# RWKV element work in pairs of 512 columns, token shift partly on ScalarE, attention banks emptied by ScalarE

## The chip, the cores and the metric

One core of a Trainium2 chip (trn2) runs the whole kernel in one launch. The metric is device time in microseconds (us): 1360.03 us, the median of 3 runs (1355.95 to 1360.05). Engine names are those of the profile: PE is TensorE, DVE is VectorE, ACT is ScalarE, POOL is GpSimd, SP is SyncE, which issues most of the transfers.

## The reference, cut to what matters

One decoder layer for 256 positions and width 2048, all in float32:

```
p = rms_norm(h, norm_mix) @ w_in                       # 16 RWKV heads x 64, and attention
p = p + (shift(p) - p) * mu                            # token shift, RWKV columns only
r, k, v, xw, xa, xg = split(p)
decay = exp(-exp(-softplus(-(w0 + tanh(xw) @ w_decay_up)) - 0.5))
a = sigmoid(a0 + xa @ a_up);  g = sigmoid(xg) @ g_up
kk = k * k_k / max(|k * k_k|, 1e-12);  k = k * (1 + (a - 1) * k_a)
state = state * decay + (state @ -kk) (kk * a)^T + v k^T ;  y = state @ r      # 256 steps
yn = layer_norm(y) ;  bonus = sum(r * k * r_k) * v
y_rwkv = (yn + bonus) * g
y_att = sparse attention (indexer, top 64 of 256 keys)
h = h + [y_rwkv, y_att] @ w_mix_out ; h = h + cross attention ; h = h + relu(..)^2 MLP
```

## The kernel before, in words

All projections go through `gemm` (L186). A weight chunk of up to 1024 columns is loaded by SP (L176, 4 buffers), ACT writes its high part `whi` (L182), DVE its low part `wlo` (L183, 3 buffers each), and PE runs three matmuls per block (high x high, high x low, low x high). The first two tenths of the program are a mixture: the stream of panels (`g_stream`: misc, k and r of head group 0, gates, v of group 0, then attention kv, qi, k and r of group 1, v of group 1, memory keys, attention q, and three parts of the output projection), the RWKV work of two groups of 8 heads (`r_group`: `rwkv_elem`, `rwkv_gram`, `rwkv_state`) and the sparse attention (`d_stream`). After about 560 us come cross attention and the MLP, which the change doesn't touch.

What the change and the steps of the prediction touch:

- **Token shift**, `shift_bank` (L340): for each PSUM bank of two channel tiles, DVE multiplies the bank by the row of norm factors into `pt` (L347, 512 columns), subtracts neighbours (L349, 512) and makes the sum with factor mu (L351, 256 columns, twice). POOL clears one column (L346). There are 12 such banks for r, k and v of both groups, and two for the misc panel.
- **Element work**, `rwkv_elem` (L441): per group two pairs of 128-channel blocks. A pair starts with the matmuls `zw`, `za` (L453) and ACT's tanh (L458, L459); sums of squares on PE (L468) give `inv` (L471, L472), spread by ACT to `inve` (L474) and turned by PE into `ss` (L509). POOL makes the log decay (L498), DVE scans it (L500), ACT takes two exponentials (L503, L505), and DVE multiplies everything into `AR` (L511, L513) and `BK` (L514, L515, L518, L519), one block of 256 columns at a time.
- **Gram matrices**, `rwkv_gram` (L529): 32 products `pg` of `BK` and `AR` (L538), which DVE masks from PSUM into `Gm` (L541); transposes `pb`, `rb`, `pv`; the result goes through DRAM (`ndd`, `Nb`), is inverted on DVE in 31 steps (`Ub`, L601, L603), and comes back through DRAM as `U`, for the first state product `p1` (L631).
- **Attention panels**, `att_panel` (L790): four banks per panel, scaled by the norm factor into SBUF, two by ACT (L799) and two by DVE (L801).

Matrix panels take PSUM banks from a pool of four (`g`), the RWKV work from two (`r`), in the order of allocation, so a panel or a product waits until the earlier owner of its bank has been read. The tile framework orders each engine's instructions by a model of time when the program is built, and each engine then runs its list in that order. The generators in `run` (L123) set the order of allocation by planned times (`yield 5.0` and the like).

Of the kernel before, what the change touches and what calls it, by code (L numbers as in the profile page):

```python
# [10 lines left out]
F32 = mybir.dt.float32  # L11
# [68 lines left out]
def hybrid_block(ctx: ExitStack, tc: tile.TileContext, I, out):  # L80
# [16 lines left out]
        return sb.tile(shape, dt, tag="s4", bufs=N4, name=name)  # L97

    def tr1(shape, name, dt=F32):
        return sb.tile(shape, dt, tag="r1", bufs=10, name=name)  # L100

    def tr2(shape, name, dt=F32):
        return sb.tile(shape, dt, tag="r2", bufs=2, name=name)

    def td1(shape, name, dt=F32):
        return sb.tile(shape, dt, tag="d1", bufs=6, name=name)
# [233 lines left out]
    def shift_bank(bank, tiles):  # L340

        n = len(tiles)
        m = max(t[0] for t in tiles)
        pt = sb.tile([P, 2, T + 1], F32, tag="pt", bufs=2, name="pt")
        df = tr2([P, 2, T], "df")
        G.memset(pt[:m, :n, 0:1], 0.0)  # L346
        V.tensor_tensor(pt[:m, :n, 1:], bank[:m, :n * T].rearrange("p (n t) -> p n t", n=n),  # L347
                        nx["bc"][:m, None, :].to_broadcast([m, n, T]), op=ALU.mult)
        V.tensor_tensor(df[:m, :n], pt[:m, :n, :T], pt[:m, :n, 1:], op=ALU.subtract)  # L349
        for a, (mm, mu, o) in enumerate(tiles):  # L350
            V.scalar_tensor_tensor(o, df[:mm, a], pc("mu", mu)[:mm], pt[:mm, a, 1:],  # L351
                                   op0=ALU.mult, op1=ALU.add)
# [47 lines left out]
    def rkv_panel(i):  # L400
# [40 lines left out]
    def rwkv_elem(g):  # L441
# [2 lines left out]
        PC = const.tile([P, NCH, GJ], F32, tag="PC", bufs=2, name="PC")  # L444
        rk = const.tile([P, 4 * GJ], F32, tag="rk", bufs=2, name="rk")
        st[g] = dict(AR=AR, BK=BK, PC=PC, rk=rk)
        for jj in range(0, GJ, 2):
            zb = [psr("zw"), psr("za")]
            for a in range(2):
                J = g * GJ + jj + a  # L450
                for i in range(2):
                    h = slice(64 * i, 64 * i + 64)
                    TE.matmul(zb[i][:, a * T:a * T + T], lora[h, J * P:J * P + P], lx[h], start=True, stop=True)  # L453
            pair, sqs = [], []
            for a in range(2):
                J = g * GJ + jj + a
                lw, a_ = tr1([P, T], "lw"), tr1([P, T], "a_")
                S.activation(lw, zb[0][:, a * T:a * T + T], AF.Tanh, bias=hw0[:, J:J + 1], scale=0.5)  # L458
                S.activation(a_, zb[1][:, a * T:a * T + T], AF.Tanh, bias=ha0[:, J:J + 1], scale=0.5)  # L459
# [3 lines left out]
                pair.append((lw, a_))  # L463
# [29 lines left out]
            for a in range(2):
                j, J = jj + a, g * GJ + jj + a
                k_, r_ = kx[g][:, j, :], rx[g][:, j, :]
                lw, a_ = pair[a]
                kp = kps[a]
                G.tensor_scalar(lw, lw, -0.5 * DEC, -0.5 * DEC, op0=ALU.mult, op1=ALU.add)  # L498
                cum = tr1([P, T], "cum")
                V.tensor_tensor_scan(cum, pc("scan"), lw, 0.0, op0=ALU.mult, op1=ALU.add)  # L500
                Pp = tr1([P, NCH, C + 1], "Pp")
                G.memset(Pp[:, :, 0:1], 1.0)
                S.activation(Pp[:, :, 1:], c3(cum), AF.Exp)  # L503
                Pi = tr1([P, T], "Pi")
                S.activation(Pi, cum, AF.Exp, scale=-1.0)  # L505
                G.tensor_copy(PC[:, :, j], Pp[:, :, C])
                ss = psr("ss")
                for t in range(2):
                    TE.transpose(ss[:, t * P:t * P + P], inve[:, 2 * a + t, :], ident)  # L509
# [280 lines left out]
    def att_panel(i):  # L790
# [523 lines left out]
```

## Time and profile before

| | before |
|---|---|
| median of 3 runs | 1360.03 us |
| profiled execution, its own time | 1358.12 us |
| span of its instructions | 1356.3 us |
| PE busy | 1318.3 us, 97% |
| DVE busy | 876.3 us, 65% |
| ACT busy | 684.2 us, 50% |
| POOL busy | 20.6 us, 2% |
| mean granted TensorE clock | 0.981 of full speed |

The profiled execution's own time is 1.8 us above its span. PE is busy nearly always, so a saving must come from the few places where PE waits or runs at its lower clock; busy time of the other engines counts only there. A share over the whole span hides these places, so the stretches are read by windows.

### The profile page before, as it was taken

The numbers are of one execution on the slowest core, as the hardware profiler recorded it, in microseconds if no ns is written. First come the engines' busy times: TensorE is split into PE (matmuls) and PEld (weight loads), VectorE is DVE, ScalarE is ACT, GpSimd is POOL, SyncE is SP. The second block draws the span as 40 slices with busy tenths as digits, with TensorE's granted clock in tenths as the row PEclk, the third lists the DMA queues.
The fourth block names the chain that finished last, engine by engine and source line by source line (L and its number), as shares of the span: only waits on it lengthen the run. The fifth ranks groups of instructions, "written<-read, shape, count | busy, mean of one in ns | idle before, by whom it ended". The sixth has DMA issues, their size and how long they took to land.

```text
span 1356.3 us, 20607 instructions
## 1 busy us (share of the span) xinstructions
PE 1318.3 (97%) x7989; PEld 1141.1 (84%) x7989; DVE 876.3 (65%) x1459; ACT 684.2 (50%) x1009; POOL 20.6 (2%) x69
## 2 busy tenths in 40 slices
PE   7999799997999999999999999999999999999997
PEld 7999788987978778887888888888888888888886
DVE  5477676599777765776665656555656556565655
ACT  5545334546544663666553544445445344363453
POOL 0001000001000000000000000000000000000000
PEclk9999699998899999999999999999999999999999
DMA  8844345334657425565666666666666666666663
GB/s 262 284 133 139 99 156 160 107 109 131 201 153 235 129 83 153 183 219 173 184 186 199 189 190 195 189 190 192 191 190 191 195 187 187 199 188 191 195 190 123
DMA packets 81489, 239.06 MB, mean 176 GB/s; under 512 B 20752, under 2 KB 20880, under 8 KB 81392
## 3 DMA queue, kind: packets, MB, share of 16 engines
q1 hardware_dynamic: 76864, 237.15, 57.4%
q8 instruction: 62, 1.02, 0.3%
q10 hardware_dynamic: 4528, 0.61, 0.3%
q14 instruction: 35, 0.29, 0.1%
HBM read 234.58 MB, written 3.15 MB: 175 GB/s over the span
## 4 chain that ended last, share of the span: by engine, by line
PE 85%; DMA 5%; DVE 5%; ACT 3%; issue 1%; SPq 0%; DVEq 0%; ACTq 0%; POOL 0%; POOLq 0%
PE gb L216 17%; PE gb L222 13%; PE gb L223 13%; PE gb L224 13%; PE gb L218 9%; PE gb L211 4%; PE gb L210 4%; PE gb L212 4%; DVE wlo L183 2%; ACT whi L182 1%; DMA x_tm<-in_x 1%; PE pg L538 1%; PE psi L858 1%; DMA raw<-in_w_mix 1%; DMA x_tm<-in_mem 1%
## 5 line engine op out<-in xcount | busy, mean ns | idle before, releaser
L183 DVE TENSOR_TENSOR wlo<-raw,whi 128x1024 fp32r<-128x1024 f32 (+2 forms) x416 | 498.4, 1200 | 365.5 <-ACT whi L182 362.5
L182 ACT ACTIVATE whi<-raw 128x1024 fp32r<-128x1024 f32 (+2 forms) x416 | 432.1, 1041 | 493.0 <-PE gb L224 249.5
L216 PE MATMUL gb<-xhl,whi 128*128 128x512 f32 x1024 | 350.4, 394 | 0.3 <-DVE hres L1045 0.3
L218 PE MATMUL gb<-xhl,wlo 128*128 128x256 f32 x1024 | 269.9, 279 | 0.0
L216 PEld LDWEIGHTS gb<-xhl,whi 128*128 128x128 f32 x1024 | 189.4, 188 | 38.5 <-ACT xhl L265 0.7
L218 PEld LDWEIGHTS gb<-xhl,wlo 128*128 128x128 f32 x1024 | 192.7, 188 | 6.4
L224 PE MATMUL gb<-whi,ul 128*128 128x512 f32 x480 | 186.9, 389 | 0.0
L223 PE MATMUL gb<-wlo,uh 128*128 128x512 f32 x480 | 186.9, 389 | 0.0
L210 PE MATMUL gb<-xhl,whi 128*128 128x256 f32 x560 | 163.5, 294 | 7.6 <-ACT whi L182 6.2
L211 PE MATMUL gb<-xhl,whi 128*128 128x256 f32 x560 | 163.1, 292 | 0.0
L212 PE MATMUL gb<-xhl,wlo 128*128 128x256 f32 x560 | 160.2, 291 | 2.2 <-DVE wlo L183 2.2
L222 PE MATMUL gb<-whi,uh 128*128 128x512 f32 x480 | 132.2, 389 | 0.0
L210 PEld LDWEIGHTS gb<-xhl,whi 128*128 128x128 f32 x560 | 109.8, 196 | 10.7 <-ACT whi L182 6.2
L212 PEld LDWEIGHTS gb<-xhl,wlo 128*128 128x128 f32 x560 | 109.0, 197 | 4.3 <-DVE wlo L183 2.8
L211 PEld LDWEIGHTS gb<-xhl,whi 128*128 128x128 f32 x560 | 110.2, 197 | 1.7 <-DVE xhl L312 0.9
L222 PEld LDWEIGHTS gb<-whi,uh 128*128 128x128 f32 x480 | 90.1, 188 | 18.8
L224 PEld LDWEIGHTS gb<-whi,ul 128*128 128x128 f32 x480 | 90.1, 188 | 18.7
L223 PEld LDWEIGHTS gb<-wlo,uh 128*128 128x128 f32 x480 | 90.1, 188 | 18.6
L223 PE MATMUL gb<-wlo,xhl 128*128 128x512 f32 (+1 forms) x224 | 82.5, 373 | 0.7 <-DVE wlo L183 0.6
L224 PE MATMUL gb<-whi,xhl 128*128 128x512 f32 (+1 forms) x224 | 81.9, 370 | 0.0
L222 PE MATMUL gb<-whi,xhl 128*128 128x512 f32 (+1 forms) x224 | 65.1, 376 | 0.2 <-ACT whi L182 0.2
L1045 DVE TENSOR_TENSOR hres<-hres,gb 128x512 f32<-128x512 f32 x92 | 57.4, 680 | 0.1
(390 smaller groups left out, 1425.7 us busy)
## 6 DMA issues: line engine op xcount, KB each, us to landing
raw<-in_w_up SPq DMA_DIRECT2D x128, 512.0 KB, 4.2
raw<-in_w_dn SPq DMA_DIRECT2D x128, 512.0 KB, 4.2
raw<-in_w_rkv SPq DMA_DIRECT2D x48, 512.0 KB, 3.9
raw<-in_w_att SPq DMA_DIRECT2D x32, 512.0 KB, 4.2
raw<-in_w_mix SPq DMA_DIRECT2D x32, 512.0 KB, 3.7
raw<-in_w_att SPq DMA_DIRECT2D x16, 296.0 KB, 3.1
rawx<-in_memT SPq DMA_DIRECT2D x8, 512.0 KB, 3.9
raw<-in_w_ck SPq DMA_DIRECT2D x8, 512.0 KB, 3.7
```

Of the source, the lines that this page charges most:

```text
L182: S.activation(hi[:, :n], raw[:, :n], AF.Copy)
L183: V.tensor_tensor(lo[:, :n], raw[:, :n], hi[:, :n].bitcast(F32), op=ALU.subtract)
L210: TE.matmul(o, wh, xh, start=st_, stop=False, skip_group_check=True)
L211: TE.matmul(o, wh, xl, start=False, stop=False, skip_group_check=True)
L212: TE.matmul(o, wl, xh, start=False, stop=last, skip_group_check=True)
L216: TE.matmul(o, wh, xt[(k + a) // 4][:, (k + a) % 4].rearrange("p s t -> p (s t)"), start=first, stop=False, skip_group_check=True)
L218: TE.matmul(o[:, :T], wl, xh, start=False, stop=last, skip_group_check=True)
L222: TE.matmul(o, xh, wh, start=first, stop=False)
L223: TE.matmul(o, xh, wl, start=False, stop=False)
L224: TE.matmul(o, xl, wh, start=False, stop=last)
L538: TE.matmul(pgs[e][:, j * P:j * P + P], BK[half[e], c, j].rearrange("p a t -> p (a t)"), AR[half[e], c, j].rearrange("p a t -> p (a t)"), ...
L1045: V.tensor_tensor(dst, dst, banks[b * 2 + t], op=ALU.add)
```

## The change

- **Token shift.** The low and high parts of the formula change places: the sum is now p·(1-mu) + shift(p)·mu. DVE writes the scaled bank straight into its destination (512 columns, L343 of the changed file), ACT multiplies it by mu into the next column of `q` (twice), and DVE adds with the factor `omu` = 1-mu (twice). The subtraction and the tile `pt` are gone.
- **Element work in pairs.** All tensors of a pair are 512 columns wide. The channel factors are applied by ACT (`gk`, `f_`, the first half of `AR`, and `BK`'s copies), r_k goes into the matmul's operand `srk`, and what is left for DVE is one kind of instruction, the product of two tensors of 512 columns. The two `ss` tiles become one. The pair has a `yield` in the middle.
- **Attention panels.** ACT empties all four banks.
- The small tiles' buffers change from 10 and 2 to 8 and 5.

```
     def shift_bank(bank, tiles, both=None):
+        if both is not None:
+            V.tensor_tensor(both, bank.rearrange("p (n t) -> p n t", n=2),
+                            nx["bc"][:, None, :].to_broadcast([P, 2, T]), op=ALU.mult)
+        q = tr2([P, 2, T], "q")
+        G.memset(q[:, :, 0:1], 0.0)
+        for a, (m, mu, o) in enumerate(tiles):
+            if both is None:
+                V.tensor_tensor(o, bank[:m, a * T:a * T + T], nx["bc"][:m], op=ALU.mult)
+            S.activation(q[:m, a, 1:], o[:, :T - 1], AF.Copy, scale=pc("mu", mu)[:m])
+            V.scalar_tensor_tensor(o, o, omu[:m, mu:mu + 1], q[:m, a], op0=ALU.mult, op1=ALU.add)
...
-                kp = tr1([P, T], "kp")
-                S.activation(kp, a_, AF.Identity, scale=hka[:, J:J + 1], bias=oka[:, J:J + 1])
-                V.tensor_tensor(kp, kp, kx[g][:, j, :], op=ALU.mult)
-                rkk = tr1([P, T], "rkk")
-                V.scalar_tensor_tensor(rkk, rx[g][:, j, :], pc("rk", J), kp, op0=ALU.mult, op1=ALU.mult)
...
+            G.tensor_scalar(flat(lw), flat(lw), -0.5 * DEC, -0.5 * DEC, op0=ALU.mult, op1=ALU.add)
...
+                S.activation(gk[:, a], f_[:, a], AF.Identity, scale=hkk[:, J:J + 1], bias=hkk[:, J:J + 1])
+                S.activation(f_[:, a], f_[:, a], AF.Identity, scale=hka[:, J:J + 1], bias=oka[:, J:J + 1])
+                S.activation(AR[:, :, jj + a, 0, :], c3(kx[g][:, jj + a, :]), AF.Copy, scale=nkk[:, J:J + 1])
+            for a in range(2):
+                V.tensor_tensor_scan(lw[:, a], pc("scan"), lw[:, a], 0.0, op0=ALU.mult, op1=ALU.add)
+            Pp = tr2([P, 2, T], "Pp")
+            S.activation(flat(Pp), flat(lw), AF.Exp)
+            S.activation(flat(lw), flat(lw), AF.Exp, scale=-1.0)
...
+            V.tensor_tensor(lw, lw, k2, op=ALU.mult)
+            V.tensor_tensor(AR[:, :, two, 1, :], cj(r2), cj(Pp), op=ALU.mult)
+            o = AR[:, :, two, 0, 1:]
+            V.tensor_tensor(o, o, cj(Pp)[:, :, :, 0:C - 1], op=ALU.mult)
+            for e in range(2):
+                h = half[e]
+                S.activation(BK[h, :, two, 1 - e, :], cj(f_)[h], AF.Copy)
+                V.tensor_tensor(BK[h, :, two, e, :], cj(gk)[h], ss[h], op=ALU.mult)
+            for s in range(2):
+                o = BK[:, :, two, s, :]
+                V.tensor_tensor(o, o, cj(lw), op=ALU.mult)
+            rkk = tr2([P, 2, T], "rkk")
+            V.tensor_tensor(rkk, f_, k2, op=ALU.mult)
+            V.tensor_tensor(rkk, rkk, r2, op=ALU.mult)
+            yield 5.0
...
-                V.scalar_tensor_tensor(AR[:, :, j, 0, :], c3(k_), nkk[:, J:J + 1], Pp[:, :, 0:C],
-                                       op0=ALU.mult, op1=ALU.mult)
-                V.tensor_tensor(AR[:, :, j, 1, :], c3(r_), Pp[:, :, 1:], op=ALU.mult)
-                V.scalar_tensor_tensor(a_, a_, 1.0, Pi, op0=ALU.add, op1=ALU.mult)
-                V.scalar_tensor_tensor(a_, k_, hkk[:, J:J + 1], a_, op0=ALU.mult, op1=ALU.mult)
-                for e in range(2):
-                    h = slice(64 * e, 64 * e + 64)
-                    V.tensor_tensor(BK[h, :, j, e, :], c3(a_)[h], c3(ss[:, :T])[h], op=ALU.mult)
-                    V.tensor_tensor(BK[h, :, j, 1 - e, :], c3(kp)[h], c3(Pi)[h], op=ALU.mult)
...
-                if t == 0:
-                    S.activation(o, src, AF.Copy, scale=nx["rs"][:, t:t + 1])
-                else:
-                    V.tensor_scalar(o, src, nx["rs"][:, t:t + 1], None, op0=ALU.mult)
+                S.activation(o, src, AF.Copy, scale=nx["rs"][:, t:t + 1])
```

The order in which the engines run their lists changes in many places, of which two matter below. First PE, where the kv panel's matmuls (`gb`, 296 columns) meet the end of group 0's element work and its gram products `pg`. Before, the panel ends and the gram follows with nothing between:

```order
L224 MATMUL gb_1433<-whi,xhl 128x296
L538 MATMUL pg_1373<-AR,BK 128x128 x4
L538 MATMUL pg_1374<-AR,BK 128x128 x4
L538 MATMUL pg_1452<-AR,BK 128x128 x4
L538 MATMUL pg_1453<-AR,BK 128x128 x4
L538 MATMUL pg_1482<-AR,BK 128x128 x4
L538 MATMUL pg_1483<-AR,BK 128x128 x4
L538 MATMUL pg_1512<-AR,BK 128x128 x4
L538 MATMUL pg_1513<-AR,BK 128x128 x4
L567 MATMUL pb<-par,BK 128x128 x16
L579 MATMUL rb<-par,rke 128x128 x8
L588 MATMUL pv<-par,vp 128x128 x12
```

Now the second pair's whole element work stands on PE with four panel matmuls between its steps, when the panel has run 14 of its 192:

```order
L222 MATMUL gb_1393<-whi,xhl 128x296
L524 MATMUL sst<-srk,rkk 128x2 x4
L464 MATMUL zw<-lx,lora 128x256 x2
L223 MATMUL gb_1392<-wlo,xhl 128x296
L224 MATMUL gb_1392<-whi,xhl 128x296
L223 MATMUL gb_1393<-wlo,xhl 128x296
L224 MATMUL gb_1393<-whi,xhl 128x296
L464 MATMUL za<-lx,lora 128x256 x2
L479 MATMUL sst<-par,sq 128x2 x4
L502 MATMUL ss<-par,inve 128x128 x4
L524 MATMUL sst<-srk,rkk 128x2 x4
L545 MATMUL pg_1335<-AR,BK 128x128 x4
```

The other 174 panel matmuls now stand between the gram products and the transposes (`pb`, `rb`, `pv`), in runs of 15 to 25 such as this one:

```order
L224 MATMUL gb_1395<-whi,xhl 128x296
L545 MATMUL pg_1415<-AR,BK 128x128 x4
L545 MATMUL pg_1444<-AR,BK 128x128 x4
L222 MATMUL gb_1395<-whi,xhl 128x296
L223 MATMUL gb_1395<-wlo,xhl 128x296
L224 MATMUL gb_1395<-whi,xhl 128x296
L222 MATMUL gb_1392<-whi,xhl 128x296
```

Second DVE, at the same place. The panel's last two banks (`gb_1394`, `gb_1395`) are those that hold the v panel until the token shift has read it (`vp<-gb`). Before, DVE read them (into `pt`) soon after the v panel's end:

```order
L183 TENSOR_TENSOR wlo<-raw,whi 128x592
L347 TENSOR_TENSOR pt<-gb_957,rsx_bc 128x2x256
L183 TENSOR_TENSOR wlo<-raw,whi 128x592
L347 TENSOR_TENSOR pt<-gb_958,rsx_bc 128x2x256
L482 TENSOR_TENSOR kp<-kp,kx 128x256
```

Now this stands behind the second pair's element work and the first `Gm`:

```order
L512 TENSOR_TENSOR BK<-gk,ss 64x4x2x64 x2
L506 TENSOR_TENSOR AR<-rx,Pp 128x4x2x64
L508 TENSOR_TENSOR AR<-AR,Pp 128x4x2x63
L518 TENSOR_TENSOR rkk<-f__1187,kx 128x512
L505 TENSOR_TENSOR lw<-lw,kx 128x512
L519 TENSOR_TENSOR rkk<-rkk,rx 128x512
L515 TENSOR_TENSOR BK<-BK,lw 128x4x2x64 x2
L526 COPY rk<-sst 128x8
L548 TENSOR_TENSOR Gm_1333<-pg_1335,par 128x512
L343 TENSOR_TENSOR vp<-gb_961,rsx_bc 128x2x256
L343 TENSOR_TENSOR vp<-gb_962,rsx_bc 128x2x256
```

So 174 of the kv panel's matmuls are free to run beside the gram, but only after these rows.

## Rows read from the trace of the kernel before

**Rows 1.** The page, parts 1 and 2: busy time, and the clock in 40 slices

```profile
PE 1318.3 (97%) x7989; PEld 1141.1 (84%) x7989; DVE 876.3 (65%) x1459; ACT 684.2 (50%) x1009; POOL 20.6 (2%) x69
PEclk9999699998899999999999999999999999999999
```

**Rows 2.** Windows: stretch, length, busy by engine (instructions), granted clock, DMA share, GB/s

```profile
100.00:150.00 50.00, 45.90 (x309) 42.57 (x309) 39.17 (x80) 25.22 (x46) 5.03 (x19) 0.94 0.50 147
150.00:200.00 50.00, 47.03 (x214) 39.66 (x214) 32.85 (x80) 18.50 (x28) 1.30 (x5) 0.82 0.37 109
300.00:350.00 50.00, 42.73 (x315) 40.35 (x314) 46.28 (x109) 30.18 (x60) 7.83 (x19) 0.90 0.50 157
350.00:400.00 50.00, 47.60 (x285) 41.14 (x284) 35.15 (x77) 24.64 (x43) 0.86 (x4) 0.90 0.52 155
```

**Rows 3.** Windows of 5 us, same columns (PE, PEld, DVE, ACT, POOL, then clock)

```profile
140.00:145.00 5.00, 1.83 (x11) 1.62 (x11) 4.92 (x9) 1.06 (x1) 0.00 (x0) 0.93 0.79 207
145.00:150.00 5.00, 4.89 (x26) 4.54 (x26) 4.84 (x9) 1.26 (x2) 1.26 (x5) 0.50 0.65 214
165.00:170.00 5.00, 4.15 (x14) 3.67 (x15) 4.73 (x18) 4.37 (x11) 0.00 (x0) 0.50 0.01 3
325.00:330.00 5.00, 0.68 (x4) 0.47 (x4) 4.89 (x11) 2.85 (x8) 0.00 (x0) 0.86 0.12 46
335.00:340.00 5.00, 5.00 (x30) 5.00 (x29) 4.34 (x14) 4.77 (x14) 0.41 (x1) 0.61 0.74 219
340.00:345.00 5.00, 5.00 (x46) 5.00 (x44) 4.49 (x12) 3.99 (x8) 0.11 (x1) 1.00 0.73 229
```

**Rows 4.** Waits of PE: line, whom it waited for, us in total, times, longest

```profile
PE zw L453 <- DVE BK L518: 5.5, 1, 5.5
PE pg L538 <- DVE BK L518: 3.6, 2, 3.2
```

**Rows 5.** Chain that ended last, in order of time: start, us, what

```profile
144.32 2.06 PE pg L538 x11
149.33 7.80 PE pg L538 x40
...
307.93 1.06 PE zw L453 x4
...
374.52 1.42 PE pg L538 x16
```

**Rows 6.** DVE groups by shape: count, busy us, mean ns, idle before

```profile
L347 DVE TENSOR_TENSOR pt<-gb,rsx_bc 128x512 f32<-128x512 f32 x13 | 8.9, 687 | 5.5 <-PE gb L212 5.3
L349 DVE TENSOR_TENSOR df<-pt 128x512 f32<-128x512 f32 x13 | 8.8, 680 | 0.0
...
L519 DVE TENSOR_TENSOR BK<-kp,Pi 64x256 f32<-64x256 f32 x16 | 6.7, 416 | 0.1
L500 DVE TENSOR_TENSOR_SCAN cum<-par,lw 128x256 f32<-128x256 f32 x8 | 5.4, 681 | 0.0
...
L511 DVE SCALAR_TENSOR_TENSOR AR<-kx,nkk,Pp 128x256 f32<-128x256 f32 x8 | 3.8, 479 | 0.7 <-ACT Pp L503 0.6
...
L513 DVE TENSOR_TENSOR AR<-rx,Pp 128x256 f32<-128x256 f32 x8 | 3.4, 420 | 0.0
...
L801 DVE TENSOR_SCALAR p_qi<-gb,rsxy 128x512 f32<-128x512 f32 x2 | 1.5, 748 | 0.7 <-PE gb L224 0.7
```

**Rows 7.** ACT groups by shape, same columns

```profile
L671 ACT ACTIVATE gt<-gt,par 128x256 f32<-128x256 f32 x8 | 3.8, 505 | 5.0 <-DVE bv L669 5.0
L458 ACT ACTIVATE lw<-zw,hw 128x256 f32<-128x256 f32 x8 | 3.8, 470 | 8.9 <-PE zw L453 8.9
...
L505 ACT ACTIVATE Pi<-cum 128x256 f32<-128x256 f32 x8 | 3.2, 401 | 0.0
...
L474 ACT ACTIVATE inve<-inv 128x512 f32<-128x512 f32 x4 | 2.5, 619 | 1.6 <-DVE inv L472 1.6
...
L799 ACT ACTIVATE p_qi<-gb,rsxy 128x512 f32<-128x512 f32 x2 | 1.4, 688 | 0.7 <-PE gb L224 0.7
...
L481 ACT ACTIVATE kp<-a__1030,oka,hka 128x256 f32<-128x256 f32 x1 | 0.6, 601 | 0.0
```

**Rows 8.** The line of POOL's log decay: count, duration ns min/median/max, first and last start

```profile
L498 POOL TENSOR_SCALAR lw<-lw x8: 404/405/1657, 101.7 to 336.2; 128x256 f32<-128x256 f32 x8
```

More of the change, by code (lines that the diff above doesn't have):

```diff
@@ L99, in tr1 @@
     def tr1(shape, name, dt=F32):
-        return sb.tile(shape, dt, tag="r1", bufs=10, name=name)
+        return sb.tile(shape, dt, tag="r1", bufs=8, name=name)
     def tr2(shape, name, dt=F32):
-        return sb.tile(shape, dt, tag="r2", bufs=2, name=name)
+        return sb.tile(shape, dt, tag="r2", bufs=5, name=name)
     def td1(shape, name, dt=F32):
@@ L337, in hybrid_block, with shift_bank @@
     pos_i = const.tile([P, 2], I32, name="pos_i")
[L340 to L352, printed above, removed]
+    def shift_bank(bank, tiles, both=None):
+        if both is not None:
[8 more added lines that the diff above has]
+            V.scalar_tensor_tensor(o, o, omu[:m, mu:mu + 1], q[:m, a], op0=ALU.mult, op1=ALU.add)
+    omu = const.tile([P, 27], F32, name="omu")
+    V.tensor_scalar(omu, pc("mu"), -1.0, 1.0, op0=ALU.mult, op1=ALU.add)
+    srk = const.tile([P, 8, 2], F32, name="srk")
     lx = const.tile([P, T], F32, name="lx")
@@ L378, in gates @@
     def gates():
+        V.tensor_tensor(srk, sel[:, None, :].to_broadcast([P, 8, 2]), pc("rk")[:, :, None].to_broadcast([P, 8, 2]),
+                        op=ALU.mult)
         w2 = s4([96, RW], "gup2s", F32R)
@@ L434, in rkv_panel @@
                 shift_bank(banks[hf * 2 + b],
-                           [(P, base + g * GJ + b * 2 + h, dst[:, b * 2 + h, :]) for h in range(2)])
+                           [(P, base + g * GJ + b * 2 + h, dst[:, b * 2 + h, :]) for h in range(2)],
+                           dst[:, b * 2:b * 2 + 2, :])
     st = {}
@@ L446, in rwkv_elem @@
         st[g] = dict(AR=AR, BK=BK, PC=PC, rk=rk)
+        flat = lambda t_: t_.rearrange("p j t -> p (j t)")
+        cj = lambda t_: t_.rearrange("p j (c t) -> p c j t", t=C)
+        half = [slice(0, 64), slice(64, 128)]
         for jj in range(0, GJ, 2):
+            two = slice(jj, jj + 2)
+            k2, r2 = kx[g][:, two, :], rx[g][:, two, :]
             zb = [psr("zw"), psr("za")]
@@ L451, in rwkv_elem @@
                 for i in range(2):
[L452 removed]
+                    h = half[i]
                     TE.matmul(zb[i][:, a * T:a * T + T], lora[h, J * P:J * P + P], lx[h], start=True, stop=True)
[L454 removed]
+            lw, f_ = tr2([P, 2, T], "lw"), tr2([P, 2, T], "f_")
+            sqs = []
             for a in range(2):
                 J = g * GJ + jj + a
[L457 to L459 removed]
+                S.activation(lw[:, a], zb[0][:, a * T:a * T + T], AF.Tanh, bias=hw0[:, J:J + 1], scale=0.5)
+                S.activation(f_[:, a], zb[1][:, a * T:a * T + T], AF.Tanh, bias=ha0[:, J:J + 1], scale=0.5)
                 sq = tr1([P, T], "sq")
                 S.activation(sq, kx[g][:, jj + a, :], AF.Square, scale=pc("kk", J))
[L463 removed]
                 sqs.append(sq)
+            G.tensor_scalar(flat(lw), flat(lw), -0.5 * DEC, -0.5 * DEC, op0=ALU.mult, op1=ALU.add)
             sst = psr("sst")
@@ L475, in rwkv_elem @@
             inve = inve.rearrange("p (n e) c -> p n (e c)", e=2)
-            kps, rks = [], []
+            gk = tr2([P, 2, T], "gk")
             for a in range(2):
-                j, J = jj + a, g * GJ + jj + a
-                lw, a_ = pair[a]
-                kp = tr1([P, T], "kp")
-                S.activation(kp, a_, AF.Identity, scale=hka[:, J:J + 1], bias=oka[:, J:J + 1])
-                V.tensor_tensor(kp, kp, kx[g][:, j, :], op=ALU.mult)
-                rkk = tr1([P, T], "rkk")
-                V.scalar_tensor_tensor(rkk, rx[g][:, j, :], pc("rk", J), kp, op0=ALU.mult, op1=ALU.mult)
-                kps.append(kp)
-                rks.append(rkk)
+                J = g * GJ + jj + a
+                S.activation(gk[:, a], f_[:, a], AF.Identity, scale=hkk[:, J:J + 1], bias=hkk[:, J:J + 1])
[6 more added lines that the diff above has]
+            S.activation(flat(lw), flat(lw), AF.Exp, scale=-1.0)
+            G.tensor_copy(PC[:, :, two], cj(Pp)[:, :, :, C - 1])
+            ss = psr("ss")
+            for i in range(4):
+                TE.transpose(ss[:, i * P:i * P + P], inve[:, i, :], ident)
+            ss = cj(ss.rearrange("p (j t) -> p j t", j=2))
+            V.tensor_tensor(lw, lw, k2, op=ALU.mult)
[13 more added lines that the diff above has]
+            yield 5.0
             sst = psr("sst")
@@ L489, in rwkv_elem @@
                 for t in range(2):
-                    TE.matmul(sst[:, 4 * a + 2 * t:4 * a + 2 * t + 2], rks[a][:, t * P:t * P + P], sel,
-                              start=True, stop=True)
+                    TE.matmul(sst[:, 4 * a + 2 * t:4 * a + 2 * t + 2], rkk[:, a, t * P:t * P + P],
+                              srk[:, g * GJ + jj + a, :], start=True, stop=True)
             V.tensor_copy(rk[:, 4 * jj:4 * jj + 8], sst[:, :8])
[L493 to L509, printed above, removed]
-                V.scalar_tensor_tensor(AR[:, :, j, 0, :], c3(k_), nkk[:, J:J + 1], Pp[:, :, 0:C],
-                                       op0=ALU.mult, op1=ALU.mult)
-                V.tensor_tensor(AR[:, :, j, 1, :], c3(r_), Pp[:, :, 1:], op=ALU.mult)
-                V.scalar_tensor_tensor(a_, a_, 1.0, Pi, op0=ALU.add, op1=ALU.mult)
-                V.scalar_tensor_tensor(a_, k_, hkk[:, J:J + 1], a_, op0=ALU.mult, op1=ALU.mult)
-                for e in range(2):
-                    h = slice(64 * e, 64 * e + 64)
-                    V.tensor_tensor(BK[h, :, j, e, :], c3(a_)[h], c3(ss[:, :T])[h], op=ALU.mult)
-                    V.tensor_tensor(BK[h, :, j, 1 - e, :], c3(kp)[h], c3(Pi)[h], op=ALU.mult)
-                yield 5.0
+            yield 5.0
     def copy_on(e, o, i):
```

## The prediction

> **What bounds the kernel now.** I read the page first. PE is busy 97% of the span and its granted clock is full except in a few slices [rows 1]; DVE is at 65% and ACT at 50%. The change leaves PE's work as it is, so the time can only come from places where PE idles or runs at the lower of its two clock levels (half). Windows of 50 us show where these are; a stretch's loss is its length minus PE's busy time, plus one minus the granted clock times the length. In 100 to 150 that is 4.1 + 3.0 = 7.1 us, in 150 to 200 3.0 + 9.0 = 12.0: 19.1 for head group 0. In 300 to 350 it is 7.3 + 5.0 = 12.3, in 350 to 400 2.4 + 5.0 = 7.4: 19.7 for group 1 [rows 2]. Together 38.8 us, the most that the change can win if PE's work stays.
>
> Windows of 5 us then show what each loss is. In 140 to 145 PE is busy 1.83 of 5 us while DVE is busy 4.92: the kv panel is over and the gram products wait for the last `BK`. From 145 on PE is busy, but at half clock, and still is in 165 to 170 [rows 3]. The list of waits names it: `pg` for `BK`, 3.6 us in two [rows 4]. The chain shows what the clock costs: 11 + 40 `pg` in 144.32 to 157.1, against 16 in 1.42 us at 374.5, where the clock is full: .25 us each against .089 [rows 5]. In group 1 PE gets .68 of 5 us in 325 to 330 with DVE at 4.89; the half clock follows and has gone by 340 [rows 3]. PE waits there for one thing, `zw` of the second pair, 5.5 us behind DVE's `BK` of the pair before [rows 4]. DVE works 46.28 of 50 us in this stretch, ACT 30.18 [rows 2]. So in both places the engine that comes last is DVE.
>
> **Part by part.** *Element work on DVE.* Before, a block of 256 columns costs 2 x .42 + 3 x .48 + .42 + 4 x .42 + .68 (scan) = 5.06 us [rows 6], 10.1 a pair. After, a pair has two scans and nine products of 512 columns, for which the subtraction at .68 and the PSUM product at .69 stand [rows 6]: 1.36 + 6.2 = 7.6. This is 2.5 less per pair, 10 over four pairs. Were a 512 product as dear as two of 256 (.84), it would be 1.1 per pair; I take .69, since L349 has that very shape.
>
> *Token shift on DVE.* Per bank .69 + .68 + 2 x .48 = 2.33 before, .69 + .96 = 1.65 after: .68 less, 8.2 over twelve banks. *Attention panels:* six banks leave DVE, at most 6 x .75 = 4.5 us.
>
> *ACT.* The shift adds two products of 256 columns, .505 each as `gt` [rows 7], 1.0 per bank and 12 in all. A pair was 6.2 us: four tanh .47, two squares .47, `inve` .62, two Identity .60, four exponentials .40. It becomes 9.3: two more Identity, two `AR` products of .505, two `BK` copies of 512 columns at .62, and two exponentials of 512 at .62 for the four [rows 7]. That is 3.1 per pair, 12.4 in all; with the banks (.69 each, six of them) ACT gets some 29 us more while DVE loses 22. As ACT is far from full, the sum takes nothing for this by itself, but the hand-overs count below.
>
> By the rule that multiplications belong on VectorE and not on ScalarE (the Trainium skill, "ScalarE: Activation LUTs", "Rules for kernel authors"), the change moves work the wrong way: adding the two engines' times would give about 7 us more. A 256 product does take .505 on ACT against .42 on DVE [rows 6, 7], so the trace agrees with the sign, but in the stretches that count DVE is the fuller engine [rows 2], and I don't add them.
>
> *Group 0, the order.* Of the kv panel only 18 of 192 matmuls can run before the `v` banks are free, and these are read by DVE after the second pair's elements and the first `Gm`. So the second pair stands nearly alone on PE. Its chain is `zw` and `za` 1.06 each (the 1.06 us of four [rows 5]), two tanh .94, `inve` .62, two Identity 1.2, nine products 6.2, eight `pg` .7, `Gm` .69 and two bank reads 1.4: 13.9 us, with hand-overs about 16. PE has some 6 us of work in it, so it idles about 10, and a half clock behind it costs some 3 more (from group 1's, which ends within about 10 us). In return the gram no longer runs alone: the 174 free panel matmuls stand between its steps. So a loss of 13 stands in place of 19.1: **gain 6**. The ends: nothing, if the chain is as long as the old loss; 12, if the last part of the first pair and the panel's 18 matmuls cover half of the chain. Nothing excludes a loss, which is the third rival. The first `U` chain starts about as late as before, and `p1` now stands behind 146 of 192 qi matmuls instead of 182; I give it nothing, because 40 more matmuls cover it and DVE has less to do.
>
> *Group 1, the order.* DVE loses 2 x 2.5 + 6 x .68 = 9.1 us where it is the bound, so `zw`'s 5.5 us and part of the 5 + 5 us of clock loss could go. But ACT rises by 6 x 1.0 + 2 x 3.1 = 12.2, from 30.2 to 42.4 of 50, and the work goes from DVE to ACT and back in each shift bank and four times in each pair. **I take 5**, about half of 9.1; the ends are 9.1 with the clock back as well (up to 14) and a loss of 3 (second-last rival).
>
> *Attention banks.* ACT needs 4 x .69 = 2.8 us for four banks where two engines needed 1.5. The banks end one behind the other, so this is covered by the next panel's matmuls: 0. Uncovered it is 1.3 x 3 panels = 3.8 us. *Log decay:* POOL now takes 512 columns at once, before the scan in place of twice 256 at .40 [rows 8]: 0, since it runs beside squares and `inve`. *Buffers:* 8 and 5 in place of 10 and 2; no row bears on a shortage, so 0.
>
> **The sum.** Profiled execution 1358.1 (its span 1356.3) - 6 - 5 = **1347 us**. The median of the runs is 1360.0, 1.9 above this execution, a seventh of a percent; I don't correct for it.
>
> **Rivals.** *1. DVE's relief comes through fully.* Group 0 gains 12 and group 1 its 9 to 14, as the new interleaving keeps the clock up: 1358.1 - 12 - 13 = 1333 us. For it: DVE is the last one at every wait [rows 3, 4]. Against it: 16 us of nearly bare chain in group 0.
>
> *2. POOL's decay becomes a link.* One of eight took 1657 ns against a median of 405 [rows 8]. If 512 columns next to DVE's products took twice that, 3.3, instead of .8, each pair is later by 2.5 us, 10 in all, and of the 11 won 1 or 2 is left: 1356 us, no change. It decides from some 2 us per decay on. Against it: seven of eight were quick. The Trainium skill ("GPSIMD Engine Reference", "8. Key points") says that this engine shares SBUF interfaces with VectorE and contends with instructions of two SBUF inputs, and the change makes nearly all DVE work that kind; the one long row fits, no run yet tells why it was long.
>
> *3. Slower: the clock stays down behind the bare chain.* Behind the wait at 140 the half clock lasted to 170 at least, although PE was busy over 4 of 5 us in the windows shown [rows 3]. If it does so after the new chain, with panel and gram both at half for some 30 us, PE loses 15 more than the 3 I count, plus a chain longer by 4: 1347 + 19 = 1366 us. It decides from some 17 us beyond the forecast on. Against it: in group 1 the clock was back by 340, when a panel ran beside the RWKV work [rows 3], and now a panel does so in group 0 too.
>
> *4. ACT becomes the last one in group 1.* Its 12.2 us on the path instead of DVE's 9.1: 3 us lost where I take 5 won, 1358.1 - 6 + 3 = 1355 us. For it: 42.4 of 50 us. Against it: this still leaves it emptier than DVE was.
>
> **How the numbers follow.** The forecast (1340 to 1354) gets .47, the first rival (1325 to 1340) .25, POOL .08, the clock .12, ACT .08. The range 1332 to 1360 leaves out the clock's .12 and the lower part of the first, some .06. About 0.3%, 4 us, is what a measurement of this kernel can tell from no change. Faster by more is the forecast and the first rival, .72; within it the second and the fourth, .16; slower the third, .12.
>
> **What would show it.** Right: the subtraction L349 gone; DVE about 22 us less over the span, ACT 29 more; PE's busy time at full clock the same; in group 0 one stretch of about 16 us in which PE is busy less than half, ahead of the kv panel's main part, and after it a gram at full clock; in 300 to 350 DVE below 42 us and no wait of `zw` above 2 us. Wrong: a half clock of over 15 us behind that stretch, a decay on POOL above 2 us in each pair, PE waits in group 1 that end with ACT's `BK` or `q`, or a new long wait for `p1`.

## The result, and the profile after

The changed kernel takes 1349.49 us (median of 7 runs, 1347.73 to 1354.18) against 1355.95 for the kernel before beside it (7 runs, 1355.25 to 1360.05): a ratio of 0.9948, 95% interval 0.9927 to 0.9969, so 4 to 10 us faster. The two profiled executions lie 10.4 us apart (1358.1 and 1347.7), because that of before is 2 us above the median of these seven and that of after is the fastest of its seven. The forecast, 11 us from 1358.1, was made on that scale; the medians give 6.5.

The page of the changed kernel, busy line and clock, answers to [rows 1]:

```profile
PE 1313.1 (98%) x7989; PEld 1137.0 (84%) x7989; DVE 857.3 (64%) x1398; ACT 708.8 (53%) x1058; POOL 16.6 (1%) x53
PEclk9997999998899999999999999999999999999999
```

DVE has 19.0 us less to do, ACT 24.6 more. The windows of 50 us, columns as in [rows 2]:

```profile
100.00:150.00 50.00, 43.77 (x303) 41.32 (x302) 29.97 (x50) 24.75 (x45) 4.57 (x14) 0.86 0.34 89
150.00:200.00 50.00, 49.41 (x314) 42.22 (x313) 39.11 (x90) 25.38 (x37) 0.58 (x1) 1.00 0.69 205
300.00:350.00 50.00, 45.20 (x327) 42.56 (x327) 42.36 (x82) 37.45 (x75) 3.47 (x8) 0.88 0.55 175
350.00:400.00 50.00, 48.94 (x252) 40.57 (x252) 33.55 (x76) 23.39 (x36) 1.38 (x5) 0.91 0.52 154
```

Read as in the prediction, group 0 loses 6.2 + 7.0 and .6 + 0 = 13.8 us where it lost 19.1, and group 1 4.8 + 6.0 and 1.1 + 4.5 = 16.4 where it lost 19.7. Windows of 5 us show the shape:

```profile
110.00:115.00 5.00, 3.73 (x22) 2.71 (x21) 1.53 (x4) 2.61 (x6) 0.62 (x1) 1.00 0.24 61
115.00:120.00 5.00, 0.40 (x4) 0.16 (x2) 4.25 (x7) 4.47 (x9) 1.65 (x8) 0.64 0.00 0
120.00:125.00 5.00, 4.64 (x25) 4.60 (x25) 2.35 (x6) 0.63 (x1) 1.59 (x5) 0.50 0.00 2
125.00:130.00 5.00, 5.00 (x22) 4.78 (x21) 3.90 (x8) 1.70 (x4) 0.00 (x0) 0.50 0.16 23
130.00:135.00 5.00, 5.00 (x41) 4.71 (x40) 3.43 (x5) 2.33 (x4) 0.00 (x0) 0.99 0.41 125
...
315.00:320.00 5.00, 0.54 (x3) 0.30 (x2) 4.94 (x10) 4.96 (x11) 0.00 (x0) 0.78 0.40 109
320.00:325.00 5.00, 4.95 (x18) 4.22 (x18) 5.00 (x12) 1.46 (x5) 0.00 (x0) 0.50 0.68 211
325.00:330.00 5.00, 5.00 (x27) 4.69 (x27) 3.61 (x8) 2.73 (x7) 0.62 (x1) 0.69 0.82 290
```

The first five rows are the bare chain of group 0's second pair: PE has nothing in 115 to 120, then the gram at half clock, and from 130 the gram beside the kv panel at full clock, where [rows 3] had half clock to 170. The last three are group 1: idle for 4.5 us, then half clock. A second half clock of theirs (348.5 to 358.8) lies on group 1's gram, as one did before (359.3 to 369.6). The list of PE's waits tells for whom, and it isn't `zw` any more [rows 4]:

```profile
PE sst L524 <- DVE rkk L519: 5.0, 1, 5.0
PE gb L211 <- DVE xhl L312: 3.1, 1, 3.1
...
PE gb L210 <- ACT xhl L311: 1.4, 1, 1.4
```

`xhl` here is the operand of the next panel (memory keys), which ACT makes at L311 and DVE at L312. The timeline of the changed kernel (start, us, engine, what) shows what DVE does in this stretch:

```profile
316.38 0.69 DVE L343 TENSOR_TENSOR vp<-gb,rsx_bc 128x512 f32<-128x512 f32 x1
...
316.99 0.68 DVE L505 TENSOR_TENSOR lw<-lw,kx 128x512 f32<-128x512 f32 x1
317.59 1.22 DVE L183 TENSOR_TENSOR wlo<-raw,whi 128x1024 fp32r<-128x1024 f32 x1
318.72 0.68 DVE L343 TENSOR_TENSOR vp<-gb,rsx_bc 128x512 f32<-128x512 f32 x1
...
319.52 0.47 DVE L312 SCALAR_TENSOR_TENSOR xhl<-rawx,par,xhl 128x256 fp32r<-128x256 f32 x1
319.92 0.68 DVE L519 TENSOR_TENSOR rkk<-rkk,rx 128x512 f32<-128x512 f32 x1
```

PE takes its list in order, and the operand stands on DVE behind the shift of v, an element product and a weight split. A few panel matmuls later in PE's list `sst` needs `rkk`, whose last product (the last row above) ends at 320.6, so without the wait for `xhl` PE would have stood nearly as long for that. The stall of group 1 has changed its name more than its length.

The new instructions' durations, DVE, ACT and POOL by shape as in [rows 6, 7]:

```profile
L512 DVE TENSOR_TENSOR BK<-gk,ss 64x512 f32<-64x512 f32 x8 | 5.5, 682 | 1.8 <-ACT gk L491 1.7
L515 DVE TENSOR_TENSOR BK<-BK,lw 128x512 f32<-128x512 f32 x8 | 5.1, 681 | 0.0
...
L350 ACT ACTIVATE q<-kx,par 128x255 f32<-128x255 f32 x8 | 3.6, 496 | 0.6 <-DVE kx L343 0.6
...
L475 POOL TENSOR_SCALAR lw<-lw 128x512 f32<-128x512 f32 x4 | 2.6, 642 | 58.7 <-ACT lw L469 58.7
```

**Two ways to count the gain.** The windows count a half clock in idle time as well, so their sum is too large. With half of the half-clock time in which PE was busy, counted from the two levels in the traces, and all of the idle time, the loss is 18.4 us before and 11.7 changed in 100 to 200, 18.2 and 15.0 in 280 to 400, 3.5 and 2.7 in 400 to 640: 6.7, 3.2 and .8 us less, 10.7 in all. In 280 to 400 only idle time fell, from 9.7 to 5.9 us; the half clock lasted 20.5 us in both traces.

The other way is a second clock for the program. ACT splits the 416 weight chunks in the same sequence in every kernel; the start of a given split tells how far a program has come. The 53rd (fifth of the qi panel; the expectations call it the first) lies behind group 0's gram, the 70th between the two groups, the 105th behind group 1's gram, the 171st in the part that the change doesn't touch. Single rows of the two timelines, before and then changed, for the 70th and the 105th:

```profile
227.93 1.06 ACT L182 ACTIVATE whi<-raw 128x1024 fp32r<-128x1024 f32 x1 [1.73 <-PE gb L211]
399.43 1.06 ACT L182 ACTIVATE whi<-raw 128x1024 fp32r<-128x1024 f32 x1 [1.66 <-PE gb L224]
```

```profile
221.83 1.06 ACT L182 ACTIVATE whi<-raw 128x1024 fp32r<-128x1024 f32 x1 [2.20 <-issue]
390.63 1.06 ACT L182 ACTIVATE whi<-raw 128x1024 fp32r<-128x1024 f32 x1 [1.66 <-PE gb L224]
```

Against the kernel before, the changed one is 8.4 us ahead at the 53rd (168.9 and 177.3), 6.1 at the 70th, 8.8 at the 105th, 10.7 at the 171st (628.3 and 639.1) and 10.5 at the end. Between the 53rd and the 70th PE is busy throughout at full clock in both kernels, so nothing is lost there: the 53rd stands at a place where the two lists have done a different amount of other work. By the 70th group 0 gives 6.1 of the 10.5 us, the stretch to the 105th 2.7 and the rest 1.7 to 1.9, which agrees with the first count. This is one pair of traces, with 4 us more between them than the medians have. `e3_banks` below, whose PE order in both groups is the old one, runs 1.4 us quicker than the kernel before between the 70th and the 105th, so a microsecond or two in one stretch tells nothing.

### The profile page after: what moved, and what is told of

It is laid out like the page before. It is cut to its first block, busy times and chain, and to the rows that moved or that the text cites. A ratio compares the mean times of both kernels' runs of the same rounds, so it can differ in the third digit from the quotient of the medians.

```text
span 1345.8 us, 20558 instructions
## 1 busy us (share of the span) xinstructions
PE 1313.1 (98%) x7989; PEld 1137.0 (84%) x7989; DVE 857.3 (64%) x1398; ACT 708.8 (53%) x1058; POOL 16.6 (1%) x53
## 4 chain that ended last, share of the span: by engine, by line
PE 88%; DVE 4%; DMA 3%; ACT 3%; issue 1%; SPq 0%; POOL 0%; DVEq 0%; ACTq 0%; POOLq 0%
PE gb L216 18%; PE gb L222 13%; PE gb L223 13%; PE gb L224 13%; PE gb L218 9%; PE gb L210 4%; PE gb L211 4%; PE gb L212 4%; DVE wlo L183 1%; PE pg L545 1%; ACT whi L182 1%; DMA par<-in_par 1%; PE psi L862 1%; DMA raw<-in_w_mix 1%; PE gb L1136 1%
## 5 line engine op out<-in xcount | busy, mean ns | idle before, releaser
L211 PE MATMUL gb<-xhl,whi 128*128 128x256 f32 x560 | 163.3, 293 | 3.1 <-DVE xhl L312 3.1
L224 PE MATMUL gb<-whi,xhl 128*128 128x512 f32 (+1 forms) x224 | 82.7, 371 | 0.0
L222 PE MATMUL gb<-whi,xhl 128*128 128x512 f32 (+1 forms) x224 | 68.5, 373 | 1.1 <-ACT p_kv L805 0.6
```

The lines of the kernel that those rows point to most:

```text
L211: TE.matmul(o, wh, xl, start=False, stop=False, skip_group_check=True)
L222: TE.matmul(o, xh, wh, start=first, stop=False)
L224: TE.matmul(o, xl, wh, start=False, stop=last)
```

## The experiments

All ratios are to the kernel before, timed together with the run (its median lay between 1355.95 and 1357.44), with 95% intervals; rows compare by their ratios. The columns on order are from the list of PE's instructions: how many of the kv panel's 192 matmuls stand ahead of the second pair's `zw`, of the first and of the last of group 0's gram products. The split is the 53rd. Where group 0 has the same code it varies by 1.1 (`changed` and `h1_extra`) to 1.5 us (the four `f` runs), and between kernels of different order by some 2 more, as the 70th showed.

| run | us, median | ratio | kv ahead of zw / first / last pg | split, us |
|---|---|---|---|---|
| before | 1355.95 | 1 | 76 / 192 / 192 | 177.3 |
| changed | 1349.49 | 0.9948 (0.9927 to 0.9969) | 14 / 18 / 77 | 168.9 |
| e1_shift | 1363.10 | 1.0055 (1.0036 to 1.0075) | 14 / 18 / 71 | 171.8 |
| e2_pairs | 1357.94 | 1.0009 (0.9994 to 1.0024) | 27 / 27 / 74 | 176.9 |
| e3_banks | 1357.67 | 1.0010 (0.9997 to 1.0024) | 76 / 192 / 192 | 176.9 |
| h0_extra | 1354.65 | 0.9993 (0.9975 to 1.0011) | 14 / 18 / 71 | 174.6 |
| h1_extra | 1370.91 | 1.0115 (1.0092 to 1.0139) | 14 / 18 / 77 | 170.0 |
| e4_shift_later | 1347.97 | 0.9945 (0.9923 to 0.9967) | 14 / 124 / 192 | 165.9 |
| e5_pairs_later | 1353.03 | 0.9972 (0.9957 to 0.9988) | 27 / 100 / 183 | 171.3 |
| f1_later | 1343.80 | 0.9905 (0.9887 to 0.9923) | 21 / 100 / 185 | 163.3 |
| f2_both | 1353.52 | 0.9983 (0.9967 to 1.0000) | 21 / 100 / 185 | 164.8 |
| f3_seven | 1342.87 | 0.9891 (0.9873 to 0.9910) | 21 / 100 / 185 | 164.7 |
| f4_four | 1345.30 | 0.9902 (0.9886 to 0.9918) | 21 / 100 / 185 | 163.5 |

### The parts alone

`e1_shift` puts the new `shift_bank` and its call into the kernel before, `e2_pairs` the new `rwkv_elem` (with `srk`), `e3_banks` this:

```
-                if t == 0:
-                    S.activation(o, src, AF.Copy, scale=nx["rs"][:, t:t + 1])
-                else:
-                    V.tensor_scalar(o, src, nx["rs"][:, t:t + 1], None, op0=ALU.mult)
+                S.activation(o, src, AF.Copy, scale=nx["rs"][:, t:t + 1])
```

> The kernel before with the new token shift alone (element work and attention banks as before). My theory: the gain of the change sits in the order around group 0's second pair and in DVE's time in group 1, and the shift brings only DVE's 12 x .68 = 8.2 us, of which at most the 6 banks of group 1 lie where DVE is last: 0 to 4 us faster than before, group 0's loss (idle plus clock in 100 to 200) still near 19. Rival, DVE's time alone counts: the shift is 8 of 22 us, so over a third of the 6.5 us gain, in both groups. Rival, ACT's added 12 us stand on the path: up to 4 us slower.

> The kernel before with the element work in pairs alone (old token shift, old attention banks; small tiles' buffers 6 and 5, the shift's own tile single). My theory: most of the gain is here, 5 to 8 us faster than before, and group 0 shows a gram that runs beside the kv panel at full clock. Rival, DVE's time alone: 10 of 22 us, so some 3 us faster.

> The kernel before with the attention banks emptied by ScalarE alone. My theory: no change, within 2 us, since the next panel's matmuls cover the banks. Rival: the four banks in a row on ACT hold the next panel, up to 3.8 us slower.

No part gains alone, and the shift loses. The theory that the pairs carry the gain fell, and so did the one that DVE's time counts wherever it is saved. The order columns show why: each of the first two already moves group 0 to the new order, with the gram beside the kv panel, and with a bare chain: 16 us without a panel matmul in the shift alone (112.6 to 128.7), as in the changed kernel, and 22 in the pairs alone (111.3 to 133.1). For the pairs alone, stretch 100 to 150, columns as before:

```profile
100.00:150.00 50.00, 40.90 (x236) 36.94 (x237) 29.94 (x52) 19.75 (x37) 5.21 (x15) 0.73 0.20 53
```

That is 9.1 us idle and a clock of .73, which eats what the gram gives back (176.9 against 177.3). The shift alone is 5.4 us ahead at the 53rd split, 4.2 behind at the 105th and 7.6 behind at the 171st. The largest wait in between is in group 1, between its elements and its gram:

```profile
350.00:355.00 5.00, 1.67 (x7) 1.31 (x8) 4.86 (x11) 4.97 (x10) 0.00 (x0) 0.92 0.68 224
355.00:360.00 5.00, 5.00 (x20) 3.71 (x19) 3.53 (x12) 1.48 (x4) 0.00 (x0) 0.50 0.55 170
```

PE waits there 4.4 us for the next panel's first weight split, which stands on ACT behind exponentials, shift products and norms; ACT is busy 4.97 of 5 us. Half clock then lasts to 370 and beyond (.50 in 365 to 370), with the gram in it. The list of waits in 340 to 360:

```profile
PE gb L222 <- ACT whi L182: 4.4, 1, 4.4
```

So the rival that ACT's work stands on the path is true here, in one place; behind the 105th split its list has a wait of 1.9 us for group 1's output (`yh`), the late end of the same group. The attention banks cost nothing that can be told (0.9997 to 1.0024), as the sum had it.

### Is the bare chain what group 0 still pays?

`f1_later` changes one number of the changed kernel; `e4_shift_later` does the same to `e1_shift`, `e5_pairs_later` to `e2_pairs` with 24:

```
-        yield (10.0, 10.0)[g]
+        yield (14.0, 10.0)[g]
```

> The changed kernel with one number changed: group 0's element work begins 4 us later in the planned order (14 for 10), so that the v panel's banks are read before the second pair's elements and the kv panel runs beside them. My theory, that the bare chain between 111 and 130 costs 13 us because kv has no banks: these 13 us go for the larger part, 5 to 10 us faster than the changed kernel, about 1341. Rival, the chain hides nothing and the clock falls anyway, where the transposes now stand alone behind the panel: within 2 us of the changed kernel. Rival, the later gram makes the state's first product late: some us slower, with a new wait there.

> The kernel before with the new token shift alone, and group 0's elements 4 us later in the planned order (14 for 10), as in the run that did the same to the changed kernel. Theory, order is what counts: the kv panel runs beside the old element work, no bare chain, and the qi panel's first weight split is at about 163 to 167, as early as with the pairs, 5 to 9 us ahead of the shift alone (171.8); group 1 stays as in the shift alone, so about 1356. Rival, DVE's 5 us less in group 0's pairs are needed to end the elements in time: the gram comes late, half of it alone behind the panel at half clock, and the split is at 171 or later.

> The kernel before with the element work in pairs alone (old shift, old attention banks), and group 0's elements later in the planned order (24 for 10, the first number that puts the v panel's banks ahead of the second pair). Theory, order decides group 0 and DVE's time only what is left: no bare chain, the qi panel's first weight split at 163 to 167 where the pairs alone had 176.9, and the whole some 8 us faster than the pairs alone, about 1347 to 1351. Rival, the pairs alone were no gain because ACT's longer links slow each pair: then the split stays above 172 even in this order.

With the v panel's banks read ahead of the second pair, its chain stands among kv matmuls (15, 34 and 30 of them between its steps). `f1_later`, windows, the last two rows from the end of the mixture (which takes about 560 of 1356 us, four tenths of the program and not two):

```profile
100.00:150.00 50.00, 49.28 (x363) 45.73 (x362) 35.26 (x58) 27.79 (x48) 5.11 (x14) 1.00 0.49 138
150.00:200.00 50.00, 48.40 (x227) 39.15 (x227) 36.58 (x86) 24.50 (x36) 0.00 (x0) 1.00 0.59 170
...
515.00:520.00 5.00, 2.40 (x12) 1.31 (x10) 3.47 (x8) 1.45 (x4) 0.00 (x0) 1.00 0.63 210
520.00:525.00 5.00, 5.00 (x15) 3.98 (x16) 0.38 (x1) 0.00 (x0) 0.00 (x0) 0.66 0.00 0
```

No half clock is left in group 0, and its loss falls from 13.8 to 2.3 us by windows (11.7 to 2.4 with half clock counted only where PE is busy); the split comes 5.6 us earlier, and the median is 5.7 us below the changed kernel's, at the lower end of the 5 to 10 expected. So the bare chain has a price, of which some 6 us arrive in the time. The loss falls by more: half clock counted half, PE is busy some 5 us longer in `f1_later`, and where, wasn't settled. The shift alone tells the same without the pairs: with the order right it is at 165.9 and 1348.0 us, 15 us below the shift in the old place (`e1_shift`), 8 below the 1356 expected, and level with the full change. The pairs alone get 5 us from the order (1353.0, split 171.3), not the 8 expected, and neither their theory (163 to 167) nor their rival (above 172) has the split. A bare stretch is left there: with 24, nothing stands between `ss` and `sst` of the first pair, and half clock follows to 129.6:

```profile
115.25 1.21 PE L522 MATMUL sst<-srk,rkk 128*128 128x2 f32 x8 [4.19 <-DVE rkk L517]
```

At the end `f1_later` is held by something new. It is 20.9 us ahead of the kernel before at the 129th split and 14.0 at the 171st: the last projection panel waits for group 1's output (`yh`, whose list entry is the first below), which isn't in the changed kernel's list.

```profile
PE gb L222 <- ACT yh L753: 1.9, 1, 1.9
```

### What a microsecond of DVE costs in either group

Both add to the changed kernel four products of 512 columns per pair that change nothing, `h0_extra` in group 0's second pair, `h1_extra` in both pairs of group 1:

```
             V.tensor_tensor(rkk, rkk, r2, op=ALU.mult)
+            for _ in range(4 if g == 0 and jj == 2 else 0):
+                V.tensor_tensor(rkk, rkk, rkk, op=ALU.max)
```

> The changed kernel with four more products of 512 columns on DVE (each the maximum of a tile with itself) in group 0's second pair, 4 x .69 = 2.8 us; the order on PE stays the same up to the first gram products. My theory: DVE's products are links of the bare chain, so the qi panel's first weight split comes 2 to 3 us later than in the changed kernel (168.9) and the whole is 2 to 3 us slower. Rival, DVE has time to spare there, since ACT's links alternate with its own: under 1 us.

> The changed kernel with the same four products more in each pair of group 1, 2 x 2.8 = 5.5 us of DVE. As predicted (DVE is the last engine in group 1, its 9 us less are worth 5): some 5 us slower than the changed kernel, with wider idle in 300 to 350. My theory now: what holds PE in group 1 is where the memory panel's operand stands in DVE's list, not DVE's sum of work, so 0 to 2 us slower, or either way as this order falls out.

In group 0, 2.8 us of DVE move the split by 5.7 us and the median by 5.2, twice the 2 to 3 expected: the wait for `rkk` grows from 5.0 to 8.7, and the half clock lengthens from 13.7 to 20.5 us.

```profile
PE sst L526 <- DVE rkk L521: 8.7, 1, 8.7
```

So in this bare chain a microsecond of DVE cost about two. It is one run, whose order behind the first gram products changed as well (71 for 77), and the intervals of the two ratios allow anything from under one to over three. In group 1 both forecasts missed: 5.5 us of DVE cost 21 (medians), of which the trace has 20.2 us by the 105th split. The list of PE's instructions changed with it: between the steps `zw`, `za`, `ss` and `sst` of the second pair stood 23, 30 and 81 panel matmuls; now it is 16, 5 and 4. The memory panel had run ahead, and the second pair of group 1 is bare:

```profile
345.00:350.00 5.00, 1.64 (x6) 0.83 (x5) 2.94 (x6) 4.44 (x9) 0.32 (x1) 0.76 0.87 291
350.00:355.00 5.00, 2.82 (x8) 1.92 (x8) 3.48 (x11) 4.97 (x10) 0.76 (x2) 0.50 0.37 118
355.00:360.00 5.00, 0.69 (x2) 0.29 (x2) 4.97 (x11) 3.45 (x8) 0.10 (x1) 0.50 0.00 0
360.00:365.00 5.00, 2.05 (x9) 2.07 (x10) 2.87 (x6) 0.00 (x0) 0.00 (x0) 0.50 0.00 0
```

PE is busy 7.2 of 20 us. This run can't price DVE's time in group 1 at an unchanged order; that stays open.

### The order in group 1

All three have group 0's elements at 14; group 1's stand at 25 (`f2_both`), 7 (`f3_seven`) and 4 (`f4_four`) for 10.

> The changed kernel with both groups' elements later in the planned order (14 and 25 for 10 and 10), so that in group 1 the v panel's shift and the memory panel's operand stand on DVE ahead of the elements. Theory, order in group 1 too: idle and clock loss of 300 to 350 (5.9 + 6.5 with group 0 alone moved) fall below 4 together, and the whole is 3 to 8 us faster than that run's 1343.8. Rival, the later group 1 makes the state and with it the output projection late: the idle comes back after 450, and the whole is the same or slower.

> The changed kernel with group 0's elements at 14 and group 1's at 7 in the planned order (14 and 10 in the best run so far, 1343.8). Theory: in that run the last projection panel waits for group 1's output (2.6 us idle in 515 to 520, then half clock), so an earlier group 1 takes up to 4 us off: 1339 to 1343. Rival: the earlier elements of group 1 meet the v panel's shift and the memory panel's operand on DVE, the gram runs partly bare, and what is won at the end is lost in 300 to 400: 1344 to 1350.

> The same with 14 and 4: the gram products of group 1 then all stand with no panel matmul between them. Theory, a bare gram costs half clock and idle: slower than 14 and 7 by 3 us or more. Rival, the earlier end of group 1 pays for it: the same or faster.

Later is worse, as the rival had it: 25.5 us ahead of the kernel before at the 105th split, 5.1 at the 171st, with the late state and attention in the list (`pTp` for DVE's `sm`, 3.6 us, among others). Earlier makes no difference that the intervals can tell: 1342.9 and 1345.3 beside 1343.8. The wait for group 1's output is gone in both (in `f4_four` 24 of the 32 gram products of group 1 ran with no panel matmul between them, not all as expected), and in its place stands the bare chain of group 1, in `f3_seven`:

```profile
PE sst L524 <- DVE rkk L519: 6.0, 1, 6.0
```

The version to keep is 14 with 10, 7 or 4, all about 0.5% below the changed kernel.

## Why the prediction was right, and where it was not

**Right: the sign, the time, and how group 0 changes.** The forecast of 1347 (1332 to 1360) met 1349.5. Its bare stretch of about 16 us is there: from 111.1 to 127.0 PE has no panel matmul, and from 130 the gram beside the panel runs at full clock. The gain from it was put at 6 us; the traces give 6.1 to 6.7. No wait for `p1` appears.

**Partly luck.** The gain forecast was 11 us; the medians give 6.5 with 4 to 10 in the interval, and only the pair of traces has 10.5. It fits that well because the terms miss in both directions: 6 and 5 were put for the groups and nothing behind them, where the traces have 6.1 to 6.7, 2.7 to 3.2 and 1 to 2. In group 0 the idle time was put at 10 us and is 6.8, the clock at 3 and is 4.9 (7.0 by windows). The 16 us of the chain are a sum of other links than the forecast's. From the chain that ended last in the changed kernel (start, us, what):

```profile
111.75 0.63 POOL lw L475
112.41 1.27 DVE lw L495 x2
...
120.36 1.84 PE sst L524 x8
122.20 4.86 PE pg L545 x24
```

The log decay, put at 0 because it would run beside the squares and `inve`, is a link of .6 us, and the two scans behind it are one of 1.3 that the chain of the forecast left out. Seven products stand ahead of `sst`, 4.5 us together, in place of nine at 6.2. And `sst` and the first gram products take 6.7 us at half clock where .7 stood for `pg`, and .69 + 1.4 for `Gm` and the bank reads. The clock of the old gram was also read too high: [rows 5] lists 51 of the 64 products, which all ran between 144.3 and 157.1, .20 us each and not .25.

**Too high: "I take 5" for group 1.** The step counted 9.1 us less on DVE where DVE is the bound, and took half, with a part of the clock loss. The traces have about 3 (2.7 and 3.2), and none of it from the clock. DVE did fall, from 46.3 to 42.4 of 50 us (below 42 was named as a sign), and `zw`'s 5.5 us went; but the step never asked what is late next. It was the memory panel's operand, 4.5 us on ACT and DVE, with the same half clock behind it. The last 1 to 2 us came after 400, where idle fell from 2.9 to 2.0 us over 400 to 600; the prediction had nothing there.

**The costs.** A 512 product takes .68 (taken: .69), with no difference between 64 and 128 partitions; the shift's product on ACT .50 (.505); DVE in all 19.0 less (22), ACT 24.6 more (29). The sums added durations, while busy time counts neighbours that overlap once: eight of 681 ns are 5.1 us busy above, not 5.4. These were the sure part, and they decided least: the shift alone saves 6.2 us of DVE for 7.5 more on ACT and is .55% slower with the element work at 10 and .55% faster at 14.

**The rivals.** *DVE's relief in full* fell in group 1 and at the bare chain; the interleaving that it named is what `f1_later` then gave in group 0 (13 us below the kernel before, half of its 25). *POOL's decay*: four of .62 to .72 us, no long one. But three of the four ran while DVE did nothing, and the fourth overlapped .2 us of a DVE instruction, so the changed kernel hardly tried it. Other traces did, and they name what the one row of 1.66 us lay beside: a weight split on DVE, an instruction on the two tensors `raw` and `whi`. In `e2_pairs` a decay of 512 columns beside two of these took 2.03 us in place of .62. Before, then `e2_pairs`:

```profile
310.68 1.21 DVE L183 TENSOR_TENSOR wlo<-raw,whi 128x1024 fp32r<-128x1024 f32 x1
310.83 1.66 POOL L498 TENSOR_SCALAR lw<-lw 128x256 f32<-128x256 f32 x1 [5.64 <-DVE m L878]
...
329.40 2.35 DVE L183 TENSOR_TENSOR wlo<-raw,whi 128x1024 fp32r<-128x1024 f32 x2
330.20 2.03 POOL L473 TENSOR_SCALAR lw<-lw 128x512 f32<-128x512 f32 x1 [11.65 <-ACT lw L467]
```

This agrees with the rule of the Trainium skill ("GPSIMD Engine Reference", "8. Key points"), but the decay doesn't always pay: where one began before an `xhl` instruction of DVE (L312), at 334.5 in the kernel before, it took its .41, and the DVE instruction .63 in place of .48. Such a meeting cost 1.2 to 1.4 us, where the rival took 2.5; that the changed kernel met none is how its lists fell out, not a step of the prediction. *The clock stays down*: it was back at 130, 10 us behind the idle stretch, with the panel beside the gram. The ground for this rival was misread, too: the old half clock to 170 was two stretches, 144.3 to 161.4 and 164.8 to 171.6, with a wait of PE for ACT between (`pv`, 2.7 us). *ACT the last one*: in 315 to 320 ACT is as full as DVE (4.96 and 4.94 of 5 us), and 1.4 of the 4.5 us end with ACT, so this rival holds a part of the truth, at the size of one wait. That multiplications on ACT are the wrong way (the Trainium skill, "ScalarE: Activation LUTs", "Rules for kernel authors") didn't decide: a 256 product is .50 there against .42 on DVE, and its sign followed the order, not the sum of engine times.

## What to carry to other kernels

Where one engine is 97% busy, a change to the helpers counts by what it does to the list of that engine: look for the chain that stands there with nothing between its links, and price it as idle plus the half clock behind it. A microsecond added to such a chain cost about two here, while some 5 us of DVE beside a panel (39.9 us busy in 100 to 150 in `e4_shift_later`, 35.3 in `f1_later`) moved the split by 2.6; and when a stall is taken away, the next late operand in the queue has to be named before the gain is booked. When a scheduler orders the lists by planned times, try its few numbers again after such a change: one of them, 14 for 10, was worth nearly as much as the whole edit (.43% and .52%).

## What was not expected of the hardware

Two pairs of rows from the changed kernel's timeline show the price of the half clock on a chain's own matmuls, at full clock and at half:

```profile
108.68 0.95 PE L524 MATMUL sst<-srk,rkk 128*128 128x2 f32 x8
109.55 1.13 PE L464 MATMUL zw<-lx,lora 64*128 64x256 f32 x4
...
120.36 1.84 PE L524 MATMUL sst<-srk,rkk 128*128 128x2 f32 x8 [4.96 <-DVE rkk L519]
...
323.12 2.07 PE L464 MATMUL zw<-lx,lora 64*128 64x256 f32 x4
```

Even products of two columns take 1.9 times as long, so a bare chain pays the clock on its own links and gets later by it, which may be one way in which 2.8 us of DVE became 5.7.
